# The second MLP product of a hybrid encoder block: four pairs of row blocks in one PSUM accumulation

## The chip, the cores and the metric

The kernel runs on one core of a Trainium2 chip. A core has a matrix engine (TensorE, PE in the rows), a vector engine (VectorE, DVE), a scalar engine (ScalarE, ACT), a general engine (GpSimd, POOL) and a queue that issues most transfers (SyncE, SP). Each executes its own instructions in order and waits for the others on semaphores. SBUF is the working memory of 128 partitions, PSUM the memory into which TensorE accumulates: eight banks, each of 512 float32 per partition. The metric is the device time of one execution in microseconds (us), lower is better; the time before is a median of three runs.

## What is computed

An encoder block over 1024 tokens of width 1024: two attention branches on a normed input, gated and merged, then an MLP with a squared ReLU and a final norm. The change touches the last part alone:

```
    merged = jax.nn.sigmoid(ga) * ya + jax.nn.sigmoid(gb) * yb
    x = x + merged @ w_out[l]

    h2 = rms_norm(x, norm_mlp_g[l], NORM_EPS)
    x = x + jnp.square(jax.nn.relu(h2 @ w_ff1[l])) @ w_ff2[l]
return rms_norm(x, norm_final_g, NORM_EPS)
```

`w_ff1` is 1024 x 4096 and `w_ff2` 4096 x 1024, all in float32.

## The kernel before

**The second product.** Call F the squared ReLU (1024 tokens x 4096). The first MLP product leaves F transposed in DRAM, `f_d[n][a]` being 128 rows of it by 1024 tokens; n counts 16 pairs of such row blocks, a = 0, 1 within a pair. One pair of F (split in token halves i and in a) and the matching 256 rows of `w_ff2` (split in a and in column halves) are two 2 x 2 block matrices, and the kernel multiplies them with seven block products instead of eight: products 1 to 7, of which 5, 6, 3 and 7 take a sum or difference of F blocks, and 5, 6, 4 and 7 a difference of weight blocks. The last two pairs (14, 15) are multiplied directly, in `last_product`.

**Operands.** Each float32 operand block is split into two parts, hi (a copy by ACT, rounded to the type float32r) and lo (the rest, a subtraction by DVE or POOL), in `operand` (L1245 to L1250). One block product is then three matmuls, hi x hi, hi x lo, lo x hi (L1291 to L1293), each with a 128 x 128 stationary block and 512 moving columns. `fa` are the operands from F, `wb` those from the weights, `fs` the combinations of F blocks (DVE, in `combine`, L1254) and `ws` those of weight blocks (POOL, the same line).

**Groups.** `ff2_group` (L1257) takes two pairs at a time, seven groups in all. For each of the seven products, in the order 1, 5, 6, 3, 4, 2, 7, it prepares the operands of both pairs and then runs four accumulations j (one for each block of 128 tokens of a half), each six matmuls into one PSUM bank. The four banks of a product alternate with the next product's: four banks as two tiles of two ("S"), and four as single tiles ("T", "T", "mm", "gm"). DVE then adds each bank into a running sum in SBUF (L1301); ACT copies instead in the first group's products 1, 5 and 6 (L1299). The running sums are the tiles `sum1`, `sum5`, `sum6` and, for the other products, quarters of the result: `xb` (first four token blocks, reloaded from DRAM by L1278) and `acc` (the other four). L1334 to L1342 put the sums together at the end, 28 instructions on DVE and POOL.

**Loads.** `pair_raws` (L1225) loads a pair of F as one tile of 128 x 2048 (`fr`, three buffers over two pools) and the weight rows as two tiles of 128 x 1024 (`w2r`, three buffers each).

**Order and memory.** The program is written in the order above, but a scheduler places each engine's instructions, and tiles come free when their last reader is done. Pools lie in SBUF as on two stacks. The pool `p52` (left) follows the operands of the first MLP product, the pools `p5` and `p5r` what lay on the right, among it the tiles `c` whose stores to `f_d` are the last step of the first MLP product (`squared`, L1141). Before the change the hi and lo operands lie in `p52`, and `fs` and `ws` in `p5r`.

Of the kernel before, what the change touches and what calls it, by code (L numbers as in the profile page):

```python
# [11 lines left out]
F32 = mybir.dt.float32  # L12
# [7 lines left out]
P = 128  # L20
# [63 lines left out]
def tile_hybrid_block(ctx: ExitStack, tc: tile.TileContext, t: dict, out: bass.AP):  # L84
# [1135 lines left out]

    s52a = tc.tile_pool(name="s52a", bufs=1)
    p52 = s52a.__enter__()
    sums = {1: [p52.tile([P, 512], F32, tag=f"sum1{j}", name=f"sum1{j}") for j in range(4)]}

    def pair_raws(pairs):  # L1225

        fr, wr = {}, {}
        for n in pairs:
            pool, bufs = (p5r, 1) if n % 3 == 2 else (p52, 2)
            fr[n] = pool.tile([P, 2, S], F32, tag="fr", name=f"fr{n}", bufs=bufs)  # L1230
            wr[n] = [wp.tile([P, D], F32, tag=("wh", "wl")[a], name=f"w2r{n}_{a}", bufs=3) for a in range(2)]
# [171 lines left out]
```

## Time and profile before

| | us |
|---|---|
| median of 3 runs | 1702.39 (1696.2 to 1707.07) |
| the profiled execution | 1701.56 |
| its span, first to last instruction | 1699.8 |
| busy in the span: PE, DVE, ACT, POOL | 1569.3, 1230.8, 709.4, 712.4 |
| matmuls of the seven groups, first and last start | 1335.5, 1640.6 |

Shares over the whole span mix stages with different limits, so the stage from 1335 to 1700 is read by itself: which engine is busy all the time there, and what TensorE waits for. Two durations are told apart: that of one instruction, and the pace, the time from one start to the next, which is shorter, since instructions of one engine overlap a little (a matmul's end is modelled and overlaps the next one by much).

### The profile page before, as it was taken

What the parts mean: (1) busy time and instruction counts of PE and PEld (TensorE: products, weight loads), DVE (VectorE), ACT (ScalarE), POOL (GpSimd) and SP (SyncE); (2) the same over time, 40 slices, a digit from 0 to 9 for tenths busy, and PEclk for the clock granted to TensorE, in tenths of its full rate; (3) what the DMA queues carried; (4) which work ended last, traced back from release to release, by engine and by line L of the source; (5) the groups of instructions that cost most, each with busy time, mean ns of one, the idle gap of its engine ahead of it and who ended that gap; (6) DMA issues with size and microseconds to landing.
All of it is one profiled execution on the core that took longest, in us unless ns stands there. A gap on an engine that the chain in (4) does not pass through costs nothing. (4 is left out here: it accounts for less than half of the span.)

```text
span 1699.8 us, 22314 instructions
## 1 busy us (share of the span) xinstructions
PE 1569.3 (92%) x8216; PEld 1324.2 (78%) x8216; DVE 1230.8 (72%) x1560; ACT 709.4 (42%) x1176; POOL 712.4 (42%) x412
## 2 busy tenths in 40 slices
PE   7899989998889998999999998999999888999997
PEld 6798767776677778899879996777888677777776
DVE  5876788689688996555546548544344899999995
ACT  4432222222567774445422336345444643333322
POOL 1634545455223241112120016333333498888771
PEclk8999999999899998999999999999999999999999
DMA  6366576555855658665475432433332632222212
GB/s 203 130 207 211 169 227 227 166 179 175 267 192 191 230 192 276 186 203 187 144 250 184 137 96 73 147 120 115 113 112 93 248 137 99 99 100 99 87 38 99
DMA packets 211869, 272.36 MB, mean 160 GB/s; under 512 B 12304, under 2 KB 146608, under 8 KB 211760
## 3 DMA queue, kind: packets, MB, share of 16 engines
q1 hardware_dynamic: 207152, 254.16, 46.0%
q10 hardware_dynamic: 4608, 16.78, 2.5%
q8 instruction: 65, 1.06, 0.3%
q14 instruction: 44, 0.36, 0.1%
HBM read 184.86 MB, written 80.27 MB: 156 GB/s over the span
## 5 line engine op out<-in xcount | busy, mean ns | idle before, releaser
L1291 PE MATMUL p<-wb_h,fa_h 128*128 128x512 f32 x392 | 157.1, 402 | 21.5 <-DVE xb L1301 8.1
L1292 PE MATMUL p<-wb_l,fa_h 128*128 128x512 f32 x392 | 155.8, 397 | 4.2 <-DVE wb_l L1249 4.2
L1293 PE MATMUL p<-wb_h,fa_l 128*128 128x512 f32 x392 | 155.3, 397 | 0.0
L1291 PEld LDWEIGHTS p<-wb_h,fa_h 128*128 128x128 f32 x392 | 74.9, 191 | 44.4 <-issue 14.5
L1249 POOL TENSOR_TENSOR wb_l<-ws,wb_h 128x512 fp32r<-128x512 f32 x54 | 86.0, 1603 | 17.3 <-ACT wb_h L1248 17.3
L1292 PEld LDWEIGHTS p<-wb_l,fa_h 128*128 128x128 f32 x392 | 75.5, 193 | 20.7 <-DVE wb_l L1249 5.2
L1293 PEld LDWEIGHTS p<-wb_h,fa_l 128*128 128x128 f32 x392 | 75.3, 192 | 16.5 <-DVE fa_l L1249 0.5
L702 ACT ACTIVATE p<-sb,mn 128x1024 f32<-128x1024 f32 x64 | 71.4, 1117 | 38.3 <-DVE mn L700 24.1
L697 PE MATMUL sb<-kb,qb 128*128 128x512 f32 x256 | 74.7, 416 | 13.1 <-ACT p L702 7.6
L700 DVE TENSOR_REDUCE mn<-sb 128x1 f32<-128x1024 f32 x64 | 76.7, 1216 | 11.0 <-PE sb L697 10.7
L1249 POOL TENSOR_TENSOR wb_l<-w2r,wb_h 128x512 fp32r<-128x512 f32 x48 | 78.7, 1660 | 13.7 <-ACT wb_h L1248 13.7
L164 POOL TENSOR_SCALAR n_y<-n_ss 128x1 f32<-128x1 f32 x23 | 6.0, 261 | 186.1 <-ACT n_xn L171 183.1
L273 DVE TENSOR_TENSOR s<-w 128x512 f32<-128x512 f32 x15 | 13.5, 901 | 97.2 <-DMA w<-in_w_ff 97.2
L254 POOL TENSOR_TENSOR wt_f_l<-w,wt_f_h 128x1024 fp32r<-128x1024 f32 x15 | 36.1, 2408 | 91.6 <-ACT wt_f_h L253 91.6
L1248 ACT ACTIVATE fa_h<-fs 128x512 fp32r<-128x512 f32 x56 | 35.1, 627 | 84.9 <-issue 40.9
L1249 DVE TENSOR_TENSOR fa_l<-fs,fa_h 128x512 fp32r<-128x512 f32 x56 | 70.4, 1264 | 0.0
L811 PE MATMUL sa<-kh_a,zq 128*128 128x256 f32 x256 | 69.2, 301 | 0.0
L1248 ACT ACTIVATE fa_h<-fr 128x512 fp32r<-128x512 f32 x50 | 31.2, 626 | 90.7 <-PE p L1292 52.2
L836 DVE TENSOR_TENSOR pta<-ta,pta 128x512 fp32r<-128x512 f32 x64 | 43.8, 688 | 33.7 <-ACT pta L835 33.4
L697 PEld LDWEIGHTS sb<-kb,qb 128*128 128x128 f32 x256 | 46.4, 194 | 25.4 <-ACT p L702 11.2
L811 PE MATMUL sa<-kl_a,zq 128*128 128x256 f32 x256 | 66.1, 289 | 0.0
L1142 ACT ACTIVATE c<-c 128x512 f32<-128x512 f32 x64 | 39.6, 623 | 56.2 <-DVE c L300 50.1
(500 smaller groups left out, 5272.1 us busy)
## 6 DMA issues: line engine op xcount, KB each, us to landing
w<-in_w_in SPq DMA_DIRECT2D x32, 512.0 KB, 4.2
qk<-r ACTq DMA_DIRECT2D x32, 512.0 KB, 4.5
f<-c SPq DMA_DIRECT2D x64, 256.0 KB, 4.6
w2r<-in_w_ff SPq DMA_DIRECT2D x32, 512.0 KB
fr<-f SPq DMA_DIRECT2D x32, 512.0 KB, 6.2
w<-in_w_ff SPq DMA_DIRECT2D x30, 512.0 KB
vb<-vb SPq DMA_DIRECT2D x16, 512.0 KB, 6.9
rot<-raw SPq DMA_DIRECT2D x64, 128.0 KB, 3.8
```

The source lines that it names most:

```text
L254: eng.tensor_tensor(lo[:, :n, :], x, f(hi[:, :n, :]), op=ALU.subtract)
L697: nc.tensor.matmul(sps[:, 512 * n:512 * n + 512], q[:, z, (qb % 4) * P:(qb % 4 + 1) * P], o.k[m][:, 512 * n:512 * n + 512], start=z == 0, ...
L700: nc.vector.tensor_reduce(mn, sps, axis=AX.X, op=ALU.min)
L702: nc.scalar.activation(p, sps, AF.Exp, scale=-1.0, bias=mn, accum_out=o.zz[qb][:, m:m + 1])
L811: nc.tensor.matmul(ps[:, 0:CM], zq[:, n % 4, c, :], kk[:, c * CM:(c + 1) * CM], start=c == 0 and kk is o.kh, stop=c == NCLS - 1 and kk is ...
L836: nc.vector.tensor_tensor(view[1], tv, f(view[0]), op=ALU.subtract)
L1142: nc.scalar.activation(c, c, AF.Relu)
L1248: nc.scalar.activation(hi, x, AF.Copy)
L1249: eng.tensor_tensor(lo, x, f(hi), op=ALU.subtract)
L1291: nc.tensor.matmul(acc, ah[:, c], bh, start=i == 0, stop=False)
L1292: nc.tensor.matmul(acc, ah[:, c], bl, start=False, stop=False)
L1293: nc.tensor.matmul(acc, al[:, c], bh, start=False, stop=i == len(ops) - 1)
```

## The change

Two pairs become one operand tile, "two pairs wide" (128 x 2 x 512): hi, lo, `fs` and `ws` are made for two pairs in one instruction. Pairs 0 and 1 are a group by themselves; after it three groups take four pairs each, so that an accumulation is twelve matmuls. The product order is 1, 5, 6, 3, 7, 2, 4. Products 6, 3 and 4 don't begin a new accumulation: they go on in the banks of products 1, 5 and 7, after DVE or ACT has read these. `sum1` falls away, and what is put together at the end is four instructions of 128 x 2048. Running sums are whole tiles, and where a bank tile is two banks wide, one instruction reads both.

All `ws` move from POOL to DVE, and so do the lo parts of the weights in product 1 (`nc.vector if which == 1 ...`). Operand tiles move from `p52` to `p5` on the right, four buffers of double width for eight; the F blocks and weight blocks are loaded by block (i, j) into single-buffered tiles `ra`, `rb` in `p52` (`rb00` in another pool), with rows of 512 elements.

```diff
-    def combine(eng, x, y, op, tag, name):
-        r = p5r.tile([P, 512], F32, tag=tag, name=name, bufs=6)
-        eng.tensor_tensor(r, x, y, op=op)
-        return r
...
+        def load_a(i, j):
+            r["a", i, j] = p52.tile([P, GROUP, 512], F32, tag=f"ra{i}{j}", name=f"ra{i}{j}_{pairs[0]}")
+            for g, n in enumerate(pairs):
+                nc.sync.dma_start(r["a", i, j][:, g, :], f_d[n][j][:, 512 * i:512 * i + 512])
...
+        for kind, i, j in (("b", 0, 0), ("a", 0, 0), ("b", 0, 1), ("a", 1, 0), ("a", 1, 1), ("b", 1, 1), ("a", 0, 1), ("b", 1, 0)):
+            (load_a if kind == "a" else load_b)(i, j)
...
     def operand(x, tag, name, eng):
-        hi = p52.tile([P, 512], F32R, tag=tag + "h", name=name + "_h", bufs=8)
-        lo = p52.tile([P, 512], F32R, tag=tag + "l", name=name + "_l", bufs=8)
+        hi = p5.tile([P, 2, 512], F32R, tag=tag + "h", name=name + "_h", bufs=4)
+        lo = p5.tile([P, 2, 512], F32R, tag=tag + "l", name=name + "_l", bufs=4)
         nc.scalar.activation(hi, x, AF.Copy)
         eng.tensor_tensor(lo, x, f(hi), op=ALU.subtract)
...
+    PRODUCTS = ((1, 0), (5, 0), (6, 1), (3, 1), (7, 0), (2, 0), (4, 1))
...
-                u = combine(nc.gpsimd, x, y, ALU.subtract, "t", f"ws{which}_{n}")
...
+                nc.vector.tensor_tensor(u, x, y, op=ALU.subtract)
+            return operand(s, "a", f"fa{name}", nc.vector), operand(
+                u, "b", f"wb{name}", nc.vector if which == 1 or begin and which == 5 else nc.gpsimd)
...
+                    nc.tensor.matmul(acc, ah[:, i % 2, c], bh[:, i % 2, :], start=i == 0 and not more, stop=False, skip_group_check=bool(more))
...
-                    for d, a in reads:
-                        if pairs[0] == 0 and which in (1, 5, 6):
-                            nc.scalar.activation(d, a, AF.Copy)
-                        else:
-                            nc.vector.tensor_tensor(d, a, d, op=ALU.add)
...
+                if begin and which in (5, 6):
+                    nc.scalar.activation(to, of, AF.Copy)
+                else:
+                    nc.vector.tensor_tensor(to, of, to, op=ALU.add)
...
+    s52 = tc.tile_pool(name="s52", bufs=1, side="right")
...
+    ff2_group((0, 1), raws, 0)
+    g_fin = load_gain(p5, t["norm_final_g"], "g_fin")
+    for count, n in enumerate(range(2, NP2 - 2, GROUP)):
+        pairs = tuple(range(n, n + GROUP))
+        ff2_group(pairs, pair_raws(pairs), count + 1)
...
+    for x in (res[0][:, :, 512:1024], res[1][:, :, 0:512], sums[5]):
+        nc.vector.tensor_tensor(x, x, sums[6], op=ALU.add)
+    nc.vector.tensor_tensor(res[1][:, :, 512:1024], res[1][:, :, 512:1024], sums[5], op=ALU.add)
```

**Where instructions stand: ScalarE, at the seam between the two MLP products.** Before, the hi parts of the first group (`fa_0_h`, `fa_1_h`, `wb_1_h`) stand among the last steps on the tiles `c` (relu L1142, square L1143):

```order
L266 ACTIVATE p_15_11835<-f0f_11837 128x512 [waits PE_49]
L1248 ACTIVATE fa_0_h<-fr_11868 128x512 [waits DMAHW2_49]
L1248 ACTIVATE fa_1_h<-fr_11871 128x512 [waits DMAHW3_49]
L1142 ACTIVATE c_15_11710<-c_15_11710 128x512 [waits DVE_49]
L1142 ACTIVATE c_15_11712<-c_15_11712 128x512 [waits DMAHW6_49,DVE_49]
L1143 ACTIVATE c_15_11710<-c_15_11710 128x512 [waits Activation_49]
L1143 ACTIVATE c_15_11712<-c_15_11712 128x512 [waits Activation_49]
L1142 ACTIVATE c_15_11711<-c_15_11711 128x512 [waits DMAHW5_49,DVE_49]
L1248 ACTIVATE wb_1_h<-w2r_0_11872 128x512 [waits DMAHW5_49]
L1143 ACTIVATE c_15_11711<-c_15_11711 128x512 [waits Activation_49]
```

In the changed program the same engine has them behind the last square, and the first one waits for seven transfer queues, PE and POOL at once:

```order
L1144 ACTIVATE c_15_11705<-c_15_11705 128x512 [waits Activation_49]
L1143 ACTIVATE c_15_11828<-c_15_11828 128x512 [waits DMAHW4_49,DVE_49]
L1144 ACTIVATE c_15_11828<-c_15_11828 128x512 [waits Activation_49]
L1261 ACTIVATE fa_0_h<-ra_0_11862 128x1024 [waits DMAHW2_49,DMAHW3_49,DMAHW1_49,DMAHW4_49,DMAHW0_49,DMAHW5_49,PE_49,DMAHW7_49,Activation_49,Pool_49]
L1261 ACTIVATE wb_0_h<-rb_0_11860 128x1024
```

In SP's order the seven queues are those of the seven last stores of `c` to `f_d`: the operand tiles now lie where `c` lay, and come free with these stores.

**VectorE in the middle of a group.** Before (group of pairs 2 and 3; `sum`, `xb` and `acc` rows are reads of banks, `fa_l` lo parts, `fs` combinations):

```order
L1254 TENSOR_TENSOR fs_4_12733<-fr_12673 128x512
L1301 TENSOR_TENSOR sum_11915<-p_2_0_12383,sum_11915 128x512
L1301 TENSOR_TENSOR sum_11916<-p_2_0_12383,sum_11916 128x512
L1249 TENSOR_TENSOR fa_2_l<-fr_12297,fa_2_h 128x512
L1301 TENSOR_TENSOR sum_11917<-p_2_1_12384,sum_11917 128x512
L1301 TENSOR_TENSOR sum_11918<-p_2_1_12384,sum_11918 128x512
L1301 TENSOR_TENSOR sum_11919<-p_2_0_12437,sum_11919 128x512
L1249 TENSOR_TENSOR fa_3_l<-fr_12300,fa_3_h 128x512
```

After (group of pairs 6 to 9, from the start of its product 5; the number in a name is the first pair of the two):

```order
L1290 TENSOR_TENSOR fs_6_12825<-fs_6_12825,ra_6_12728 128x1024
L1262 TENSOR_TENSOR fa_8_l<-fs_8_12837,fa_8_h 128x1024
L1297 TENSOR_TENSOR ws_6_12827<-rb_6_12746,ws_6_12827 128x1024
L1290 TENSOR_TENSOR fs_8_12837<-fs_8_12837,ra_6_12728 128x1024
L1329 TENSOR_TENSOR xb<-p_6_0_12773,xb 128x2x512
L1297 TENSOR_TENSOR ws_8_12839<-rb_6_12746,ws_8_12839 128x1024
L1262 TENSOR_TENSOR fa_6_l<-fs_6_12825,fa_6_h 128x1024
L1329 TENSOR_TENSOR xb<-p_6_1_12774,xb 128x2x512
L1262 TENSOR_TENSOR fa_8_l<-fs_8_12837,fa_8_h 128x1024
```

Reads of banks become fewer against operand work, `ws` rows stand between them, and every row is of double width.

**SyncE, the loads of the groups.** Before (pairs 6 and 7; `fr` are pairs of F, `w2r` rows of `w_ff2`, each tile with two or three buffers):

```order
L1238 DMA fr_13047<-f_9456 128x1024
L1240 DMA fr_13047<-f_9456 128x1024
L1234 DMA w2r_1_13049<-in_w_ff 128x1024
L1234 DMA w2r_0_13051<-in_w_ff 128x1024
L1234 DMA w2r_0_13424<-in_w_ff 128x1024
L1238 DMA fr_13050<-f_9457 128x1024
```

After (group of pairs 6 to 9; `ra_6_12741` is its block of F with i = 1, j = 1):

```order
L1236 DMA ra_6_12749<-f_9453 128x512
L1250 DMA rb_6_12754<-in_w_ff 128x2x512 x2
L1236 DMA ra_6_12741<-f_9450 128x512
L1236 DMA ra_6_12741<-f_9451 128x512
L1236 DMA ra_6_12741<-f_9452 128x512
L1236 DMA ra_6_12741<-f_9453 128x512
L1250 DMA rb_10_13261<-in_w_ff 128x2x512
```

Loads by pair have become loads by block; this one stands last in its group's loads and waits for the last reader of the same tile in the group ahead.

## Rows read from the trace of the kernel before

**Rows 1.** Busy time by stretch (start:end, length; PE, PEld, DVE, ACT, POOL; clock; DMA):

```profile
1250.00:1300.00 50.00, 50.00 (x220) 41.12 (x219) 25.03 (x37) 21.89 (x32) 16.85 (x7) 1.00 0.37 114
1335.40:1640.90 305.50, 279.77 (x1179) 223.83 (x1178) 304.76 (x352) 123.12 (x226) 256.02 (x160) 0.97 0.31 115
1640.90:1699.80 58.90, 45.69 (x193) 36.68 (x191) 37.31 (x38) 10.80 (x21) 17.75 (x24) 0.93 0.18 72
```

**Rows 2.** PE timeline, the first and the last of 130 matmuls without a stop:

```profile
1436.22 0.39 PE L1293 MATMUL p<-wb_h,fa_l 128*128 128x512 f32 x1
...
1465.50 0.39 PE L1293 MATMUL p<-wb_h,fa_l 128*128 128x512 f32 x1
```

**Rows 3.** Who waited for whom, TensorE, 1335.4 to 1640.9: total us, times, longest:

```profile
PE p L1291 <- DVE xb L1301: 8.1, 5, 2.9
PE p L1291 <- DVE acc L1301: 5.7, 5, 2.4
PE p L1291 <- ACT wb_h L1248: 5.3, 3, 3.8
PE p L1292 <- DVE wb_l L1249: 4.2, 2, 2.7
PE p L1291 <- DVE sum L1301: 2.4, 1, 2.4
```

**Rows 4.** Instructions by line and shape, 1200 to 1700: count, busy us, mean ns:

```profile
L1249 DVE TENSOR_TENSOR fa_l<-fs,fa_h 128x512 fp32r<-128x512 f32 x56 | 70.4, 1264 | 0.0
L1301 DVE TENSOR_TENSOR sum<-p,sum 128x512 f32<-128x512 f32 x72 | 46.2, 676 | 0.0
L1254 POOL TENSOR_TENSOR ws<-w2r,ws 128x512 f32<-128x512 f32 x28 | 46.8, 1692 | 14.3 <-DMA w2r<-in_w_ff 13.9
```

**Rows 5.** DVE and POOL timelines: start, length, instruction:

```profile
1461.31 1.78 DVE L1254 TENSOR_TENSOR fs<-fs,fr 128x512 f32<-128x512 f32 x1
1490.98 1.87 DVE L1301 TENSOR_TENSOR sum<-p,sum 128x512 f32<-128x512 f32 x3
...
1464.20 1.74 POOL L1249 TENSOR_TENSOR wb_l<-ws,wb_h 128x512 fp32r<-128x512 f32 x1
...
1483.91 1.28 POOL L1249 TENSOR_TENSOR wb_l<-ws,wb_h 128x512 fp32r<-128x512 f32 x1
```

**Rows 6.** Instructions of 1024 columns, timeline of DVE and ACT:

```profile
1317.25 1.22 DVE L254 TENSOR_TENSOR w1a_l<-w_last,w1a_h 128x1024 fp32r<-128x1024 f32 x1 [5.66 <-ACT w1a_h L253]
1318.39 0.68 DVE L297 TENSOR_TENSOR c<-yf,u 128x512 f32<-128x512 f32 x1
...
1682.64 1.22 DVE L1356 TENSOR_TENSOR acc<-ff_last,acc 128x1024 f32<-128x1024 f32 x1 [0.70 <-PE ff_last L1350]
...
1318.82 1.06 ACT L253 ACTIVATE w1a_h<-w_last 128x1024 fp32r<-128x1024 f32 x1 [1.12 <-PE zf L245]
```

**Rows 7.** Instructions by line and shape, POOL, 1000 to 1335, DVE idle much of the time:

```profile
L254 POOL TENSOR_TENSOR w1a_l<-w,w1a_h 128x1024 fp32r<-128x1024 f32 x7 | 16.8, 2396 | 17.7 <-ACT w1a_h L253 17.7
```

**Rows 8.** The seam: timelines of ACT, POOL and SP, and a transfer's time to landing:

```profile
1332.91 0.58 ACT L266 ACTIVATE p<-f0f 128x512 f32<-128x512 f32 x1
1335.47 1.14 ACT L1143 ACTIVATE c<-c 128x512 f32<-128x512 f32 x2
...
1335.74 3.13 POOL L1254 TENSOR_TENSOR ws<-w2r 128x512 f32<-128x512 f32 x2 [21.48 <-PE f1f L245]
...
f<-c SPq DMA_DIRECT2D x19, 256.0 KB, 2.8
```

**Rows 9.** Busy time by stretch: the loads ahead of the seam, the restart of TensorE, the next loads:

```profile
1325.00:1330.00 5.00, 5.00 (x23) 4.04 (x22) 2.26 (x5) 2.47 (x5) 0.00 (x0) 1.00 0.92 327
...
1340.00:1345.00 5.00, 3.86 (x9) 3.09 (x10) 5.00 (x6) 2.75 (x6) 4.17 (x4) 0.50 0.70 257
...
1350.00:1355.00 5.00, 4.67 (x21) 3.86 (x21) 5.00 (x5) 3.76 (x8) 4.64 (x3) 1.00 1.03 420
```

**Rows 10.** PE timeline: restarts after a wait, and the pace behind the first:

```profile
1341.14 0.80 PE L1292 MATMUL p<-wb_l,fa_h 128*128 128x512 f32 x1 [2.70 <-DVE wb_l L1249]
...
1342.16 0.63 PE L1291 MATMUL p<-wb_h,fa_h 128*128 128x512 f32 x1
1342.59 0.63 PE L1292 MATMUL p<-wb_l,fa_h 128*128 128x512 f32 x1
...
1646.95 0.80 PE L1349 MATMUL ff_last<-wb_l,fa_h 128*128 128x512 f32 x1 [3.71 <-POOL wb_l L1249]
...
1660.50 0.50 PE L1348 MATMUL ff_last<-wb_h,fa_h 128*128 128x512 f32 x1 [1.82 <-DVE xb L1356]
```

More of the change, by code (lines that the diff above doesn't have):

```diff
@@ L1304, in tile_hybrid_block, with ff2_group, block, fresh @@
-    side = [0]
+    PRODUCTS = ((1, 0), (5, 0), (6, 1), (3, 1), (7, 0), (2, 0), (4, 1))
+    def ff2_group(pairs, r, count):
+        begin = pairs[0] == 0
+        couples = range(len(pairs) // 2)
+        temp = {}
+        def block(kind, i, j, c):
+            return r[kind, i, j, c]
+        def fresh(side, name, c):
+            temp[side, c] = wp.tile([P, 2, 512], F32, tag="wh" if side == "a" else "wl", name=name, bufs=3)
+            return temp[side, c]
+        def prepare(which, c):
+            name = f"{which}_{pairs[2 * c]}"
+            a = {1: (0, 0), 2: (0, 1), 4: (1, 1)}.get(which)
+            b = {1: (0, 0), 2: (1, 0), 3: (1, 1)}.get(which)
+            if a:
+                s = block("a", *a, c)
+            else:
+                s = fresh("a", f"fs{name}", c) if which in (5, 7) else temp["a", c]
+                x, y, op = {5: (block("a", 1, 0, c), block("a", 1, 1, c), ALU.add), 6: (s, block("a", 0, 0, c), ALU.subtract),
+                            3: (block("a", 0, 1, c), s, ALU.subtract), 7: (block("a", 0, 0, c), block("a", 1, 0, c), ALU.subtract)}[which]
+                nc.vector.tensor_tensor(s, x, y, op=op)
+            if b:
+                u = block("b", *b, c)
+            else:
+                u = temp["b", c] if which in (6, 4) else fresh("b" if which == 5 else "b7", f"ws{name}", c)
+                x, y = {5: (block("b", 0, 1, c), block("b", 0, 0, c)), 6: (block("b", 1, 1, c), u),
+                        4: (block("b", 1, 0, c), u), 7: (block("b", 1, 1, c), block("b", 0, 1, c))}[which]
+                nc.vector.tensor_tensor(u, x, y, op=ALU.subtract)
+            return operand(s, "a", f"fa{name}", nc.vector), operand(
+                u, "b", f"wb{name}", nc.vector if which == 1 or begin and which == 5 else nc.gpsimd)
+        target = {1: res[0][:, :, 0:512], 2: res[0][:, :, 0:512], 3: res[0][:, :, 512:1024], 4: res[1][:, :, 0:512],
+                  7: res[1][:, :, 512:1024], 5: sums[5], 6: sums[6]}
+        banks = [None, None]
+        for k, (which, more) in enumerate(PRODUCTS):
+            ops = [prepare(which, c) for c in couples]
+            if not more:
+                if (k + count) % 2:
+                    banks[k % 2] = [bank([P, 512], tag, f"p{which}_{pairs[0]}_{j}") for j, tag in enumerate(("T", "T", "mm", "gm"))]
+                else:
+                    banks[k % 2] = [bank2(f"p{which}_{pairs[0]}_{j}") for j in range(2)]
+            here = banks[k % 2]
+            for j in range(4):
+                wide = len(here) == 2
+                acc = here[j // 2][:, 512 * (j % 2):512 * (j % 2) + 512] if wide else here[j]
+                c = slice(j * P, j * P + P)
+                for i in range(len(pairs)):
+                    (ah, al), (bh, bl) = ops[i // 2]
+                    last = i == len(pairs) - 1
+                    nc.tensor.matmul(acc, ah[:, i % 2, c], bh[:, i % 2, :], start=i == 0 and not more, stop=False, skip_group_check=bool(more))
+                    nc.tensor.matmul(acc, ah[:, i % 2, c], bl[:, i % 2, :], start=False, stop=False, skip_group_check=bool(more))
+                    nc.tensor.matmul(acc, al[:, i % 2, c], bh[:, i % 2, :], start=False, stop=last, skip_group_check=bool(more))
+                if wide and j % 2 == 0:
+                    continue
+                to = target[which][:, j - 1:j + 1, :] if wide else target[which][:, j, :]
+                of = here[j // 2].rearrange("p (j n) -> p j n", j=2) if wide else acc
+                if begin and which in (5, 6):
+                    nc.scalar.activation(to, of, AF.Copy)
+                else:
+                    nc.vector.tensor_tensor(to, of, to, op=ALU.add)
```

111 lines of the change are left out of this document (29 added, 82 removed).

## Prediction, made before the changed kernel was timed

> **What bounds the kernel now.** I read the time by stretch first, then TensorE's waits, then the instructions of the engine that it waits for. In a stretch of the first MLP product TensorE is busy throughout and DVE half the time [rows 1]. In the seven groups, 1335.4 to 1640.9 (the last matmul with its pace), this turns round: DVE is busy 304.76 of 305.50 us, TensorE 279.77 [rows 1]. The reader is to see that TensorE's busy time hides the loss, as its matmuls overlap. So I take its pace: 130 matmuls in an unbroken run start 1436.22 to 1465.50, 0.227 us each [rows 2]. The groups have 7 x 7 x 4 x 6 = 1176 matmuls, 266.9 us at that pace: 38.6 of the 305.5 us are lost. Of these, 25.7 are waits that the trace names, and 16.2 of them end with a DVE read of a bank (L1301) [rows 3]; the rest is restarts and low clock. The stage is bound by DVE, which gives the banks back too late.
>
> Why is DVE full? One add from a bank takes 0.68 us, and three in a row 1.87, a pace of 0.60 [rows 4, 5]. The subtractions with both inputs in SBUF take 1.26 on average, for the same 512 columns [rows 4]. Single ones take 1.78 while POOL's run 1.74, where POOL alone needs 1.28 [rows 5]: the two wait for each other. For a period of two pairs DVE has 28 reads and 22 SBUF instructions, 50 x 0.60 = 30.0 us; the period is 305.5/7 = 43.6. The other 13.6 are waits for POOL, whose 22 instructions take 28 us by themselves: DVE stood still for 0.49 of POOL's time.
>
> **The change part by part, for one group of four pairs.**
>
> TensorE: 336 matmuls x 0.227 = 76.3 us, 10.9 a product. Their number, 1176, stays.
>
> Bank reads: 28 of 512 columns instead of 56. In one half of the products (single banks) four take 2.4 us at the pace of 0.60; in the other half two of 1024 columns take 1.22 each from start to end [rows 6], some 2.3 together. Seven products: 16.5 us, before 33.6.
>
> DVE's SBUF work: 14 `fa_l`, 8 `fs`, and now 8 `ws` and 2 `wb_l` of product 1, 32 instructions of 1024 columns. One lasts 1.22 with the next 1.14 behind it [rows 6]: 36.5 us (before, 44 x 0.60 = 26.4). DVE together: 53.0 us.
>
> POOL: 12 `wb_l` of 1024 columns at 2.40 [rows 7], 28.8 us, before 44 instructions and 56 us. If DVE stands still for the same 0.49 of that, it needs 53.0 + 14.1 = 67.1 us, under TensorE's 76.3; before, the same sum was 87.2. So TensorE becomes the bound of the group. ACT has 28 hi copies of 1.06 [rows 6], 30 us: no bound.
>
> The Trainium skill, page "SBUF — State Buffer", section "Who interferes with whom", says that of a DVE instruction with two SBUF inputs and a GpSimd instruction that reads SBUF the later one waits until the other is through. The trace agrees as far as 1.78 against 0.68 goes [rows 4, 5]. By that rule no fixed share protects DVE, and waits get longer with wider instructions; the first rival is worked out on that.
>
> Deadlines inside a group: four buffers of double width let ACT begin the operands of a product when the product two ahead of it ends, so one product time, 10.9 us, is there to make them. I walked through the group of pairs 6 to 9 with these prices, each POOL instruction holding DVE's SBUF work off. Product 5's operands are ready 9.4 us after product 1 has started, product 6's at 21.0 (wanted at 21.8 and, for its second two pairs, 23.6), product 7's and 2's in time; product 3's second `fa_l` is 1.1 us late, behind four `fs` and `ws` and two POOL instructions. I allow 1 to 3 us a group, take 2, and 0 as the lower bound.
>
> Loads: tiles `ra`, `rb` have one buffer, so a block's load waits for its last reader. The tightest is F block (1, 1): its last reader, product 4's second `fa_l`, ends 61.3 us into the group. Four transfers of 256 KB need 5 us at 257 to 420 GB/s with 2.8 to land the first [rows 8, 9]: there at 66.5. DVE wants it at 66.6. It is hidden by product 2 and the reads of its banks; without that cover DVE would stand, with product 1's lo parts behind it, and 9.2 us more of DVE work would follow before the next group can start at 77.3, some 1.5 us of slack. SP has nothing behind these loads but later loads.
>
> The seam: operand tiles now wait for the last store of `c`. Before, TensorE goes from the last `f1f` matmul straight into product 1. Now: the last `p` is there at 1333.5 [rows 8]; three adds of 0.60 and an `fs` of 1.14 on DVE bring 1336.5, the last add from its bank 1337.2 (the `f1f` product is through by 1335.7 [rows 8]); relu and square, 1.14 for two [rows 8], 1338.3; four stores issued by 1339.9, the last landed 2.8 later [rows 8], 1342.7; two hi copies, 1344.8; `fa_l` and `wb_l`, 1346.0. TensorE stands 1335.4 to 1346.0: 10.6 us. Bounds: 8.6 if the stores issue as the tiles come, 14 if the loads ahead (full DMA rate [rows 9]) hold up `fs`. After its first wait of 2.7 us in the trace the granted clock was 0.50, that is 1.2 GHz, and matmuls came every 0.43 us, about twelve of them [rows 9, 10]; I count the same, 12 x 0.20 = 2.4. In the small group (pairs 0, 1) products last 5.4 us; DVE has 17 SBUF instructions (19.4), 5 products of reads (11.8) and 5 POOL instructions to wait for (6), 37 against 38.1 on TensorE: 1 us of loss.
>
> Sum of the groups' loss: 10.6 + 2.4 + 1 + 3 x 2 = 20.0, before 38.6: 18.6 us gained.
>
> The last part: before, TensorE waits there 3.7 us on POOL's `wb_l`, behind two POOL sums, and 1.8 on DVE, behind the 28 combining instructions [rows 10]. Now four instructions of 2048 columns on DVE, some 2.3 us each, three of them under the last products. The weights' lo parts of the second column half can begin only when product 4 ends: ready 5.4 and 9.0 us after it, wanted at 3.0 and 6.8, so 4.7 us of waits. Gain 1 (0 to 3).
>
> 1699.8 - 18.6 - 1 = 1680.2 of span. The profiled execution took 1.8 more than its span, and the median of the runs is 0.8 above it: **1683 us**.
>
> **Rivals.**
>
> *DVE stays the bound.* If every POOL instruction holds DVE for its whole length, a group needs 53.0 + 28.8 = 81.8 us, 5.5 more than TensorE instead of the 2 allowed, 3 x 3.5 = 10.5, and the widest waits shift product 3, 6 and 7 by about a microsecond each: 1693 to 1697. For it: the doubled length of POOL's instructions, and margins of about 1 us in the walk. Against: a third of DVE's work reads PSUM, and such reads keep 0.68 next to a busy POOL [rows 4].
>
> *Slower: the single buffers of the loads.* If block (1, 1) lands late, DVE stands in order and all operands behind it. From 68 us into the group each us late is one on TensorE, at four seams (three groups and the last part). To be 17 us slower than before it must cost 37 us, 9.3 a seam: landing 16 us after issue instead of 5. For it: one buffer in place of three. Against: 1 MB would have to move at 75 GB/s, where the trace has 420 in a stretch of such loads [rows 9]. Time: 1720.
>
> *Better.* No loss inside the groups, 8.6 at the seam, 3 gained at the end: 1671.
>
> **How the numbers follow.** About 1% (17 us) is what a measurement of this kernel can tell from no change. TensorE as the bound, 1676 to 1690: 0.62, of which 0.50 lies under 1685.4, that is over 1% faster. Better: 0.08. DVE as the bound: 0.24, all within 1%. Slower: 0.06. Faster 0.58, within 1% 0.36, slower 0.06. The range runs from the better case to the upper end of the first rival, 1670 to 1697; the likeliest case alone is 1676 to 1690.
>
> **What would show it.** Right: in the three groups TensorE's starts are 0.227 us apart over whole products, DVE is busy some 0.88 instead of 1.00, and waits on bank reads (16.2 us before) are nearly gone. The seam shows TensorE idle for about 10 us until an ACT copy that waited for a store, and a clock of 0.50 behind it. The rivals would show as DVE busy all through with TensorE waiting for `fa_l` or `wb_l`, or as DVE idle on `ra` at the end of each group. I am wrong if the share of POOL's time that DVE waits is far from 0.49, or if the first operands come much later than 1346.

## The result, and the profile after

The changed kernel takes 1675.28 us (median of four runs, 1673.88 to 1676.8) where the kernel before takes 1702.14: a ratio of 0.9844, 95% interval 0.9811 to 0.9877. That is 1.6% faster. The forecast was 1683, with a range of 1670 to 1697 and most of its chance on a gain of over 1%.

DVE is VectorE and POOL is GpSimd. The profiled execution took 1675.33 us, with a span of 1673.5. Busy time of the changed kernel by stretch (start:end, length; PE, PEld, DVE, ACT, POOL; clock; DMA), the first two to be laid beside [rows 1]:

```profile
1332.40:1619.40 287.00, 271.86 (x1178) 223.45 (x1178) 264.83 (x196) 110.24 (x118) 129.43 (x43) 0.97 0.35 119
1619.40:1673.50 54.10, 44.20 (x193) 35.62 (x191) 28.81 (x22) 11.95 (x21) 13.38 (x19) 0.97 0.19 78
...
1400.00:1600.00 200.00, 200.00 (x884) 165.62 (x883) 191.00 (x143) 74.89 (x76) 98.56 (x33) 1.00 0.29 98
...
1343.80:1349.00 5.20, 4.89 (x11) 3.40 (x12) 5.20 (x6) 2.21 (x4) 0.00 (x0) 0.50 0.98 371
...
1386.50:1396.50 10.00, 10.00 (x37) 8.09 (x38) 10.00 (x10) 2.01 (x2) 2.41 (x1) 0.83 0.17 54
```

And one stretch of the kernel before, for the third of them:

```profile
1400.00:1600.00 200.00, 185.09 (x794) 148.62 (x792) 200.00 (x240) 74.37 (x136) 170.69 (x107) 0.99 0.28 103
```

In the same 200 us in the middle of the groups TensorE now starts 884 matmuls instead of 794, 0.226 us each, and is never idle. DVE has turned from the engine that is always busy (200.00) into one with 9 us to spare. The groups went from 305.5 to 287.0 us and the last part from 58.9 to 54.1; the remaining 3 us lie ahead of the last `f1f` matmul (run 10 comes back to them). Of the runs of the kernel before that were taken beside the experiments, one took 3038.01 us and is left out.

All restarts of TensorE in the changed kernel from there to the middle of the last part (PE timeline, idle time in brackets):

```profile
1332.20 0.40 PE L245 MATMUL f1f<-hB,w1a_l 128*128 128x512 f32 x1
...
1343.88 1.22 PE L1319 MATMUL p<-wb_h,fa_h 128*128 128x512 f32 x2 [11.28 <-DMA rb<-in_w_ff]
1345.33 0.80 PE L1320 MATMUL p<-wb_l,fa_h 128*128 128x512 f32 x1 [0.23 <-DVE wb_l L1262]
...
1348.48 0.63 PE L1321 MATMUL p<-wb_h,fa_l 128*128 128x512 f32 x1
1348.91 0.63 PE L1319 MATMUL p<-wb_h,fa_h 128*128 128x512 f32 x1
...
1380.88 0.47 PE L1319 MATMUL p<-wb_h,fa_h 128*128 128x512 f32 x1 [1.08 <-DVE acc L1329]
1386.41 0.50 PE L1319 MATMUL p<-wb_h,fa_h 128*128 128x512 f32 x1 [2.55 <-DVE acc L1329]
...
1619.11 0.39 PE L1321 MATMUL p<-wb_h,fa_l 128*128 128x512 f32 x1
...
1626.93 0.50 PE L1364 MATMUL ff_last<-wb_last_l,fa_last_h 128*128 128x512 f32 x1 [2.69 <-POOL wb_last_l L1262]
```

From 1386.41 to the last product at 1619.11 there is not one restart: three groups at TensorE's own pace. The 16.2 us of waits on bank reads of [rows 3] are down to 3.6, all of them ahead of that stretch. Most of what is left of the loss stands at the seam, where the operands wait for the stores of `c`; the trace puts TensorE's wait down to a load that had long landed, and ACT's wait, in the second row, names the store (who waited for whom; total, times, longest):

```profile
PE p L1319 <- DMA rb<-in_w_ff: 11.3, 1, 11.3
ACT fa_h L1261 <- DMA f<-c: 5.4, 1, 5.4
PE p L1319 <- DVE acc L1329: 3.6, 2, 2.5
PE ff_last L1364 <- POOL wb_last_l L1262: 2.7, 1, 2.7
```

How DVE and POOL hold each other now, by line and shape, 1332.4 to 1673.5 (count, busy us, mean ns), beside [rows 4]:

```profile
L1262 POOL TENSOR_TENSOR wb_l<-ws,wb_h 128x1024 fp32r<-128x1024 f32 x27 | 79.3, 2952 | 151.9 <-ACT wb_h L1261 112.1 <-DMA g_fin<-in_norm_final_g 39.8
L1262 DVE TENSOR_TENSOR fa_l<-fs,fa_h 128x1024 fp32r<-128x1024 f32 x28 | 57.4, 2053 | 1.8 <-ACT fa_h L1261 1.8
L1329 DVE TENSOR_TENSOR xb<-p,xb 128x512 f32<-128x512 f32 x24 | 16.0, 678 | 0.0
L1329 DVE TENSOR_TENSOR xb<-p,xb 128x1024 f32<-128x1024 f32 x12 | 14.6, 1214 | 0.3 <-PE p L1321 0.3
```

The bank reads cost what they were priced at (0.68 and 1.21 us beside a busy POOL), while a subtraction out of SBUF that lasts 1.22 alone has a mean of 2.05.

### The profile page after: what moved, and what is told of

It reads as the page before. It is cut to its first block, busy times and chain, and to the rows that moved or that the text cites. A ratio compares the mean times of both kernels' runs of the same rounds, so it can differ in the third digit from the quotient of the medians.

```text
span 1673.5 us, 21830 instructions
## 1 busy us (share of the span) xinstructions
PE 1555.3 (93%) x8216; PEld 1318.4 (79%) x8216; DVE 1185.1 (71%) x1389; ACT 695.8 (42%) x1064; POOL 574.4 (34%) x287
## 5 line engine op out<-in xcount | busy, mean ns | idle before, releaser
L1319 PE MATMUL p<-wb_h,fa_h 128*128 128x512 f32 x392 | 154.6, 395 | 14.9 <-DMA rb<-in_w_ff 11.3
L1262 POOL TENSOR_TENSOR wb_l<-ws,wb_h 128x1024 fp32r<-128x1024 f32 x27 | 79.3, 2952 | 151.9 <-ACT wb_h L1261 112.1
L1261 ACT ACTIVATE fa_h<-fs 128x1024 fp32r<-128x1024 f32 x28 | 29.6, 1056 | 95.9 <-PE p L1320 63.2
L1143 ACT ACTIVATE c<-c 128x512 f32<-128x512 f32 x64 | 39.8, 624 | 55.7 <-DVE c L300 50.0
L824 ACT ACTIVATE sm<-sm,mna 128x512 f32<-128x512 f32 x64 | 46.1, 720 | 32.2 <-DVE mna L820 31.8
L1262 DVE TENSOR_TENSOR fa_l<-fs,fa_h 128x1024 fp32r<-128x1024 f32 x28 | 57.4, 2053 | 1.8 <-ACT fa_h L1261 1.8
L835 ACT ACTIVATE pta<-ta 128x512 fp32r<-128x512 f32 x64 | 37.7, 592 | 50.3 <-PE ta L831 42.7
```

The source lines that it names most:

```text
L824: nc.scalar.activation(sm, sm, AF.Exp, scale=-1.0, bias=mn, accum_out=stat[h % 2][:, n:n + 1])
L1143: nc.scalar.activation(c, c, AF.Relu)
L1319: nc.tensor.matmul(acc, ah[:, i % 2, c], bh[:, i % 2, :], start=i == 0 and not more, stop=False, skip_group_check=bool(more))
```

## The experiments

Nine kernels stand beside the two. Each ratio is to the runs of the kernel before that were taken beside that kernel, whose medians are 1700.93 to 1702.87 us. The count is that of matmuls started from 1400 to 1600 us, and the last column is DVE's busy time there. A profile is of one execution, whose time can lie some us off the median: 1713.05 in run 1, 1701.65 in run 2, 1723.40 in run 5, 1676.99 in run 8.

| kernel | us, median | ratio to before (95%) | matmuls | DVE busy |
|---|---|---|---|---|
| before | 1702.14 | 1 | 794 | 200.00 |
| changed | 1675.28 | 0.9844 (0.9811 to 0.9877) | 884 | 191.00 |
| 1: groups of two | 1723.2 | 1.013 (1.0105 to 1.0154) | 739 | 185.55 |
| 2: groups of two, two load buffers | 1707.05 | 1.0016 (1.0000 to 1.0032) | 772 | 196.50 |
| 3: groups of two, `ws` on POOL | 1707.84 | 1.0035 (1.0015 to 1.0056) | 810 | 185.56 |
| 4: `ws` on POOL | 1683.43 | 0.989 (0.9861 to 0.9919) | 872 | 183.89 |
| 5: before, `ws` on DVE | 1717.38 | 1.0073 (1.0040 to 1.0106) | 720 | 200.00 |
| 6: no operand work on POOL | 1665.74 | 0.9789 (0.9769 to 0.9809) | 884 | 179.62 |
| 7: the same, groups of two | 1692.45 | 0.9934 (0.9908 to 0.9959) | 811 | 196.11 |
| 8: early operands at the seam | 1669.79 | 0.9818 (0.9785 to 0.9851) | 873 | 191.66 |
| 9: 6 and 8 together | 1656.12 | 0.9728 (0.9700 to 0.9756) | 884 | 179.71 |

(In kernels 4 and 8 TensorE has a few waits in that stretch, 1.71 and 1.86 us of them named. With the slower starts around them the starts come 2.6 and 2.5 us late, 12 and 11 matmuls: what they lack against 884.)

**1. Groups of two row blocks' pairs**, the rest of the change as it is.

```diff
-    GROUP = 4
+    GROUP = 2
```

> The changed kernel with GROUP = 2: products of two row blocks' pairs share a bank again, and everything else of the change stays (operands two pairs wide, ws combinations on VectorE, products that go on in another's bank). **Theory (the halved bank reads made the gain):** a stretch of four pairs of the changed kernel has 16.5 us of bank reads and 36.5 us of SBUF work on VectorE, 53.0, and was seen 72.5 us busy with the lock; twice the bank reads make 72.5 + 16.5 = 89.0 us against 76.5 us of TensorE, so VectorE is the bound again and the three stretches give back 3 x 12.5 = 37 us: 1712 us (1703 to 1720), with VectorE busy over 0.97 of the stage and idle time of TensorE on bank reads. **Rival (the wide instructions, the moved combinations and the end of the part made it):** those are all still there, so the time stays within 10 us of 1675.

Measured: 1723.2 us, 48 above the changed kernel and over the expected 1703 to 1720. In the profiled execution (1713.05) the groups took 324.8 us, from 1326.6 to 1651.4, 37.8 more than in the changed kernel, against the 37 expected. The rival falls: with every other part of the change in place the gain is gone. But DVE was not the full 0.97 busy:

```profile
1400.00:1600.00 200.00, 178.25 (x739) 141.12 (x737) 185.55 (x162) 60.30 (x61) 75.91 (x26) 0.97 0.29 96
```

It stood idle 14.4 us there, and its waits from 1400 to 1600 say on what:

```profile
PE p L1319 <- DVE acc L1329: 11.1, 6, 3.7
...
DVE fs L1290 <- DMA ra<-f: 7.5, 5, 2.7
DVE ws L1297 <- POOL wb_l L1262: 6.9, 4, 2.3
```

So groups of two halve the time for the loads as well as doubling the reads, and the run mixes the two. That asked for the next one.

**2. Groups of two with two buffers for the loads** (the blocks are half as large there, so that they fit).

```diff
-            r["a", i, j] = p52.tile([P, GROUP, 512], ..., name=f"ra{i}{j}_{pairs[0]}")
+            r["a", i, j] = p52.tile([P, GROUP, 512], ..., name=f"ra{i}{j}_{pairs[0]}", bufs=2)
...
-                        whole = p52.tile([P, GROUP, 512], ..., name=f"rb{i}{j}_{pairs[0]}")
+                        whole = p52.tile([P, GROUP, 512], ..., name=f"rb{i}{j}_{pairs[0]}", bufs=2)
```

> Groups of two as in the first of these runs (ws on VectorE, low parts of the weights on GpSimd), and the raw blocks ra and rb, which are half as large there, with two buffers each, so that a block's load need not wait for its last reader. **Theory (the bank reads make nearly all of the loss of groups of two):** in the 200 us from 1400 that kernel started 739 matmuls where the changed one started 884, a loss of 32.8 us, and VectorE waited for loads 7.5 us of it; over the seven groups that is at most 10 us: 1713 us (1708 to 1719). **Rival (the loads, with one buffer and half the time, made the loss):** 1675 to 1690.

Measured: 1707.05 us. That is a little under the expected 1708 to 1719. The loads were worth 16 us of the 48 (19 by the two ratios), more than the 10 that the waits in the trace had shown; the other 32 stay with the doubled bank reads. DVE is nearly full again:

```profile
1400.00:1600.00 200.00, 184.59 (x772) 147.89 (x771) 196.50 (x173) 63.84 (x64) 76.17 (x27) 0.97 0.28 92
```

This kernel has the wide operands, the moved `ws` and the products that go on in another's bank, and is level with the kernel before (1.0016). Taken together, those parts gain nothing without the halved reads, which they make possible. What each is worth by itself this run doesn't say.

**3. Groups of two, and `ws` on POOL as before.**

```diff
-    GROUP = 4
+    GROUP = 2
...
-                nc.vector.tensor_tensor(u, x, y, op=ALU.subtract)
+                nc.gpsimd.tensor_tensor(u, x, y, op=ALU.subtract)
```

> The changed kernel with groups of two and ws on GpSimd: what is left of the change is the wide operands, the new loads, and products that go on in another's bank. **Theory (only the halved bank reads pay; the rest is even or costs a little):** not faster than the kernel before; with 0.49 to 0.69 of standing still for GpSimd's 48 us of four pairs, VectorE comes to 33 + 27.4 + 23.5 to 33 = 84 to 93 us against 87.2 of the kernel before, 1695 to 1725. **Rival (the wide operands make the gain and the move of ws hid it in the kernel with groups of two):** under 1690.

Measured: 1707.84 us, 0.35% slower than the kernel before and 15 us faster than run 1: the move of `ws` had cost those 15 us. The rival's time, under 1690, did not come, but this kernel has the single load buffers, and DVE waits 12.3 us for `ra` from 1400 to 1600. Groups of two with `ws` on POOL and two load buffers were not run, so that the wide operands by themselves are no gain is not shown.

**4. Groups of four, `ws` on POOL.**

```diff
-                nc.vector.tensor_tensor(u, x, y, op=ALU.subtract)
+                nc.gpsimd.tensor_tensor(u, x, y, op=ALU.subtract)
```

> The changed kernel with the eight ws combinations of four pairs back on GpSimd, where the kernel before had them. **Theory (bank reads; the move of ws is a trade that costs VectorE little either way):** VectorE loses 8 x 1.14 = 9.1 us of its own and GpSimd gains 8 x 2.40 = 19.2 us, 48 us in all; with 0.69 us of standing still for each us of GpSimd, as the changed kernel shows it, VectorE comes to 43.9 + 33 = 77 us against 76.5 of TensorE, a tie: 0 to 5 us per stretch of four pairs lost, 1675 to 1690. **Rival (the move of ws off GpSimd is what made the gain):** most of the 26 us goes back, 1693 to 1702.

Measured: 1683.43 us. 18.7 us of the gain remain, so the move of `ws` is not its cause. In the middle TensorE nearly keeps its pace, with two waits of 1.48 and 0.23 us. The profile shows where most of the loss within the groups is, at the start of the first product:

```profile
1347.99 1.22 PE L1319 MATMUL p<-wb_h,fa_h 128*128 128x512 f32 x2 [13.18 <-DMA rb<-in_w_ff]
1351.61 0.79 PE L1320 MATMUL p<-wb_l,fa_h 128*128 128x512 f32 x1 [2.40 <-DVE wb_l L1262]
```

These two waits are 4.1 us longer than in the changed kernel, and the groups, 291.0 us, are 4.0 longer. Of the other 4 us of the profile, 2.2 lie ahead of the seam, where the edit changes nothing.

**5. The kernel before with `ws` on DVE**, one part of the change alone.

```diff
-                u = combine(nc.gpsimd, x, y, ALU.subtract, "t", f"ws{which}_{n}")
+                u = combine(nc.vector, x, y, ALU.subtract, "t", f"ws{which}_{n}")
```

> The kernel before with one part of the change alone: its ws combinations (512 columns wide) on VectorE in place of GpSimd. **Theory (with VectorE as the bound this is a trade):** for two row blocks' pairs VectorE takes over 8 x 0.60 = 4.8 us and GpSimd gives up 8 x 1.28 = 10.2 us, for which VectorE stood still 0.49 to 0.69 of the time, 5.0 to 7.1 us: from 0.2 us slower to 2.3 us faster per two pairs, 1686 to 1706 in all. **Rival A (the move makes the gain of the change):** 1675 to 1685. **Rival B (VectorE does not win back the lock, the added work is paid in full):** 7 x 4.8 = 34 us slower, 1730 to 1740.

Measured: 1717.38 us, 0.73% slower, which fits none of the three. Its groups took 321.8 us in the profile, 16.3 more than before, 2.3 for each two pairs. Of the 4.8 us that DVE takes over, it won back about half, where I had expected all of it. So the price of the lock is not a fixed share of POOL's time: the 10.2 us of POOL work that went gave back some 2.5 us, 0.24 of it, not 0.49. (The profiled execution is 6 us above the median, so 2.5 is rather too little.) The move costs where DVE is full or nearly so (this run, 200.00 of 200 us busy; run 1 against run 3, 185.55 and idle only on loads and POOL) and pays where DVE has time to spare (the changed kernel against run 4). That this is the reason is inferred from these pairs.

**6. No operand work on POOL.**

```diff
-                u, "b", f"wb{name}", nc.vector if which == 1 or begin and which == 5 else nc.gpsimd)
+                u, "b", f"wb{name}", nc.vector)
...
-    blocks_b = {(i, j): operand(r["b", i, j, 0], "b", f"wb_last{i}{j}", nc.gpsimd) ...
+    blocks_b = {(i, j): operand(r["b", i, j, 0], "b", f"wb_last{i}{j}", nc.vector) ...
```

> The changed kernel with the low parts of the weight operands (wb_l, wb_last_l) on VectorE in place of GpSimd, which then has no operand work in the stage. **Theory (VectorE's busy time of 72.5 us is 53.0 of work and 19.5 of standing still behind GpSimd):** VectorE takes over 12 x 1.14 = 13.7 us and loses the 19.5, so 66.7 us of four pairs, 0.87 of TensorE's 76.5; the steady stretches stay at TensorE's pace and give nothing, but the stalls that a held VectorE makes (1.08 and 2.55 us ahead of the first stretch of four pairs with about 2 us of low clock behind, 2.69 us on wb_last_l in the last part) go or shrink: 3 to 8 us faster than the changed kernel, 1667 to 1672. **Rival (the seconds on VectorE are real work and GpSimd's help is worth it):** VectorE comes to 72.5 + 13.7 = 86 us and the stage gets 28 us longer, about 1704.

Measured: 1665.74 us, 9.5 below the changed kernel, a little more than forecast. DVE does 12 instructions more in a group and is less busy:

```profile
1400.00:1600.00 200.00, 200.00 (x884) 165.62 (x883) 179.62 (x172) 70.98 (x73) 0.00 (x0) 1.00 0.30 100
```

179.62 of 200 us are 68.5 of a group's 76.3, against the 66.7 that the prices gave. This run has the lock out of the way and confirms the prices of DVE's own work within 3%. After the first product's two waits (11.51 and 0.23 us) the trace names no wait of TensorE up to the end of the last part's products. In the last part, DVE's big sums take their own time again (DVE timeline of this kernel, then of the changed one):

```profile
1616.03 1.22 DVE L1262 TENSOR_TENSOR wb_last_l<-rb,wb_last_h 128x1024 fp32r<-128x1024 f32 x1
1617.16 2.29 DVE L1356 TENSOR_TENSOR acc<-acc,sum 128x2048 f32<-128x2048 f32 x1
```

```profile
1620.90 3.78 DVE L1356 TENSOR_TENSOR acc<-acc,sum 128x2048 f32<-128x2048 f32 x1
1624.60 3.36 DVE L1262 TENSOR_TENSOR fa_last_l<-ra,fa_last_h 128x1024 fp32r<-128x1024 f32 x1
```

**7. The same in groups of two**, with two buffers for the loads: the bank reads with no lock in play.

```diff
-    GROUP = 4
+    GROUP = 2
```

> Groups of two with two buffers for the raw blocks, and the low parts of the weight operands on VectorE, so that GpSimd has no operand work and nothing holds VectorE; to be compared with the same kernel in groups of four (1665.7). **Theory (VectorE's own work, bank reads among it, against TensorE's):** four pairs cost VectorE 33 + 36.5 + 13.7 = 83.2 us against 76.3 of TensorE, 3 x 6.9 = 21 us, and a backlog of up to 7 us goes into the last part: 1686 to 1694, VectorE busy over 0.97 in the stretch from 1400 to 1600. **Rival (the lock with GpSimd, not the bank reads, made VectorE the bound):** without it groups of two cost no more than groups of four, 1664 to 1670.

Measured: 1692.45 us, inside the theory's 1686 to 1694, 26.7 us above run 6.

```profile
1400.00:1600.00 200.00, 187.04 (x811) 151.07 (x809) 196.11 (x204) 66.09 (x65) 0.00 (x0) 1.00 0.31 103
```

DVE is busy 0.98 with GpSimd's part of the row at zero. So in this form of the kernel, with POOL's work on DVE, twice the reads are enough to make DVE the bound without any lock. It was otherwise in the kernel before: by the prediction's prices DVE's own work was 30.0 us for two pairs, against 168 x 0.227 = 38.1 of TensorE, and only with the 13.6 us of waiting for POOL did it become the bound. There it was the reads and the lock together; the kernel before without POOL's operand work was not run (estimate: 22 instructions x 0.60 more on DVE, 43.2 us, no gain). TensorE's named wait in that stretch is 12.3 us on `wb_l` of DVE, not on a bank: a full DVE is late wherever its order puts the lateness.

**8. The first two products' operands in space that is free at once** (the sum buffers, and the halves of `ra` that the small group leaves empty), so that they need not wait for the last store of `c`.

```diff
-    def operand(x, tag, name, eng):
+    def operand(x, tag, name, eng, into=None):
...
+            if begin and which == 1:
+                ia, ib = [[early[w][:, h:h + 2, :] for h in (0, 2)] for w in (5, 6)]
+            elif begin and which == 5:
+                ia, ib = [[p52.tile([P, 2, 512], F32R, tag=f"ra{i}{j}1", ...) for j in range(2)] for i in range(2)]
```

> The changed kernel with the operands of the first two products of the first, small group in space that is free before the last store of c (the two sum buffers and the unused halves of the ra buffers), so that they do not wait for that store. **Theory (TensorE's 11.3 us at the seam are the wait for the store of c, through the space that the operands take):** product 1 starts within 3 us of the last f1f product, it and product 5 take 2 x 24 x 0.227 = 10.9 us in which the store lands, and a rest of 1 to 3 us stays ahead of product 6; the clock does not fall, which saves another 2 us: 7 to 11 us faster, 1664 to 1668. **Rival (the store itself comes later, since four ACT copies of 1.06 us and four VectorE subtractions of 1.14 us now run ahead of the squares that it waits for):** the idle time moves from product 1 to product 6 and 0 to 4 us are gained, 1671 to 1675.

Measured: 1669.79 us, 5.5 below the changed kernel, under the 7 to 11 expected and over the rival's 4. TensorE goes straight on from the last `f1f` product at 1337.35 to product 1 at 1337.58, which shows the cause of the 11.3 us. But three waits come behind, and their sum is 7.6 us:

```profile
1351.92 0.79 PE L1329 MATMUL p<-wb_h,fa_h 128*128 128x512 f32 x1 [3.27 <-ACT fa_h L1264]
1355.16 0.80 PE L1330 MATMUL p<-wb_l,fa_h 128*128 128x512 f32 x1 [2.45 <-POOL wb_l L1265]
1359.55 0.80 PE L1331 MATMUL p<-wb_h,fa_l 128*128 128x512 f32 x1 [1.89 <-DVE fa_l L1265]
```

Of them only the first goes back to the store (in ACT's order, where the copy at 1347.00 waits 0.44 us for it). The store itself comes later, as the rival had it: the last square on `c` ends 7.0 us after the last `f1f` product (1337.58), against 4.0 in the changed kernel (ACT timeline):

```profile
1343.95 0.63 ACT L1144 ACTIVATE c<-c 128x512 f32<-128x512 f32 x1
```

The other two are POOL and DVE, which hold each other there, and a fourth of the kind, 1.86 us, comes at 1425; I had counted the first alone. The clock fell all the same, a mean of 0.66 over 1348 to 1360. With it, TensorE's starts come 12.7 us late by 1368, where in the changed kernel they are 14.6 late by 1353 (both against 0.2265 us a start): at the seam itself the edit won 2 us. The groups took 281.8 us in the profile, 5.2 less than in the changed kernel, because the changed kernel's two waits at the end of the small group (5.8 us with the low clock behind) are gone as well, less 2.6 at 1425.

**9. Both edits together.** The edit is that of runs 6 and 8.

> The changed kernel with both of the last two edits: the first two products' operands in space that is free at once, and the low parts of the weight operands on VectorE. **Theory (the seam and the lock are two costs, and the second is also what kept the first edit below its forecast: of the 11.3 us at the seam 7.6 came back as waits of 3.27 on the store, 2.45 on GpSimd and 1.89 us on a held VectorE):** the last two of these go with GpSimd out of the stage, some 3 us of waiting on the store stays, and the clock does not fall: 5 to 9 us below the 1665.7 of the kernel without GpSimd, 1657 to 1661. **Rival (both edits remove the same stalls):** the gains do not add, 1663 to 1667.

Measured: 1656.12 us, 9.6 below run 6, a little beyond the 5 to 9. The clock fell here too (0.76 over 1345 to 1352), which I had not expected. One wait is left of the four:

```profile
1345.28 1.20 PE L1329 MATMUL p<-wb_h,fa_h 128*128 128x512 f32 x4 [2.93 <-ACT fa_h L1264]
```

At the seam TensorE's starts are 5.0 us late, against 12.7 in run 8. So the lock did eat most of run 8's gain there. This kernel beats both: 2.7% under the kernel before and 1.2% under the changed one.

**10. The kernel before once more.** No edit.

> The kernel before once more, for a second profile. **Theory (the 3 us by which the last f1f product ends earlier in the changed kernel, 1332.4 against 1335.3, are not of the change, since the code ahead of it is the same but for four GpSimd additions; the six profiles so far have the last f1f product anywhere from 1326.3 to 1337.4):** it starts somewhere else than at 1335.3 by 1 us or more, and the stretch from there to the last p product is 305 us again, within 2. **Rival (the change makes the part ahead of the seam shorter):** it starts at 1335 within 1 us.

Measured: one run of 1702.15 us, and the last `f1f` matmul stands where it stood:

```profile
1335.24 0.40 PE L245 MATMUL f1f<-hB,w1a_l 128*128 128x512 f32 x1
```

The expectation of another place missed; the stretch to the last product, 306 us, came as expected. The rival is right in part. The `f1f` matmuls with hi weights, first and last start, in the kernel before and in the changed one:

```profile
L245 PE MATMUL f1f<-hB,w1a_h x128: 392/396/397, 1007.8 to 1335.0; 128*128 128x512 f32 x128
L245 PE MATMUL f1f<-hB,w1a_h x128: 392/396/400, 1006.9 to 1332.0; 128*128 128x512 f32 x128
```

From the first to the last it is 327.2 us before, 327.7 in this run and 327.3 in run 5, but 324.3 to 326.3 in the changed kernel and the eight made from it. So about 2 of the 3 us go with the change. They are there within 43 us of the first start, where the kernel before has four POOL subtractions of blocks of the result (L1279, in `ff2_group`, placed that early) that the change drops, and that hold DVE (POOL and DVE, before; DVE, changed kernel):

```profile
1007.29 1.30 POOL L1279 TENSOR_TENSOR acc<-acc 128x512 f32<-128x512 f32 x1 [1.40 <-DVE n_xn L173]
...
1007.62 2.05 DVE L254 TENSOR_TENSOR w1a_l<-w1r,w1a_h 128x1024 fp32r<-128x1024 f32 x1
```

```profile
1006.73 1.23 DVE L254 TENSOR_TENSOR w1a_l<-w1r,w1a_h 128x1024 fp32r<-128x1024 f32 x1
```

That they are the whole of the 2 us was not tried by itself. The rest of the spread is not of the change: over all kernels here the last start lies at 1326.1 to 1337.1, and the first one already at 1001.0 to 1012.8.

## Why the prediction was right, point by point

**The bound.** Right. The groups were bound by DVE, through the reads of the banks on top of the waits for POOL, and halving the reads made TensorE the bound. Runs 1, 2 and 7 show it from the other side, with and without the lock: 32 us between run 2 and the changed kernel, 26.7 between runs 7 and 6.

**The sum of the groups' loss** was 20.0 us. It came out at 287.0 - 266.9 = 20.1, and the 18.6 us of gain at 18.5. That is closer than its terms deserve:

| term | predicted | measured |
|---|---|---|
| seam, TensorE idle | 10.6 | 11.28 + 0.23 |
| low clock behind it | 2.4 | 2.5 |
| first small group, up to 1386.41 | 1 | 1.08 + 2.55, and 1.7 of low clock |
| three groups of four pairs | 6 | 0 |

(The low clock: ten matmuls from 1343.88 to 1348.91 in 5.03 us, less 2.27 at the full pace and the 0.23; a clock of 0.83 over 10 us. The granted clock was 0.50, 1.2 GHz, from 1343.8 to 1349.0. The terms sum to 19.3; 0.8 are spread.)

The seam was right in its sum (first matmul forecast 10.6 us after the end of the `f1f` product, measured 11.45) and in its cause, but two of its steps were off, and they cancel by luck. The walk had the first hi copy 7.3 us after the `f1f` product; it came 9.4 after it (1332.43 to 1341.83). The squares ended 4.0 after it instead of 2.9, and the last store, issued at 1337.3, took about 4.5 us to the copy that waited for it, where 2.8 was forecast (ACT timeline, the last square and the first hi copy):

```profile
1335.83 0.63 ACT L1144 ACTIVATE c<-c 128x512 f32<-128x512 f32 x1
1341.83 1.06 ACT L1261 ACTIVATE fa_h<-ra 128x1024 fp32r<-128x1024 f32 x1 [5.37 <-DMA f<-c]
```

Against these 2.1 us, TensorE began right behind the two hi copies (1343.83) with hi x hi, where the walk had it wait 1.2 us more for the lo parts. The term for the groups was mis-sized by all of its 6 us. The walk let every POOL instruction hold all of DVE's SBUF work, and found product 3's second `fa_l` 1.1 us late; in the trace nothing of that arrived at TensorE. The small group's term was too small by 4. Ahead of its first wait (1.08) DVE stood 1.23 us for a load of `ra` into its single buffer, the first row of DVE below; ahead of the second (2.55) it lost its place through the lock (timelines of POOL and of DVE, changed kernel):

```profile
1381.74 2.40 POOL L1262 TENSOR_TENSOR wb_l<-ws,wb_h 128x1024 fp32r<-128x1024 f32 x1 [12.62 <-ACT wb_h L1261]
...
1437.48 3.41 POOL L1262 TENSOR_TENSOR wb_l<-rb,wb_h 128x1024 fp32r<-128x1024 f32 x1
```

```profile
1377.24 1.22 DVE L1290 TENSOR_TENSOR fs<-ra,ra 128x1024 f32<-128x1024 f32 x1 [1.23 <-DMA ra<-f]
...
1381.78 3.44 DVE L1290 TENSOR_TENSOR fs<-ra,ra 128x1024 f32<-128x1024 f32 x1
1385.14 1.21 DVE L1329 TENSOR_TENSOR acc<-p,acc 128x1024 f32<-128x1024 f32 x1
...
1438.54 3.43 DVE L1262 TENSOR_TENSOR fa_l<-ra,fa_h 128x1024 fp32r<-128x1024 f32 x1
```

POOL started 0.04 us earlier, DVE stood still until its 2.40 were over, and the read behind gave the bank back at 1386.35: TensorE restarts at 1386.41. In run 6, without POOL's work, the loads ahead are issued 9 us earlier (1360.99 instead of 1370.23) and neither wait is there.

**DVE's standing still.** The share of 0.49 was too low, which the prediction had named as a sign of being wrong; the bound held because a margin was left. DVE is busy 191.00 of 200 us, 72.9 of a group's 76.3 us or 0.95, where 67.1 or 0.88 was forecast. With run 6 for its own work (68.5 less the 12 x 1.14 that it took over, 54.8) it stood still 18.1 us of POOL's 28.8, 0.63. Had it been 0.75 the group would have turned to DVE's side (54.8 + 0.75 x 28.8 = 76.4). The first rival, that every POOL instruction holds DVE for its whole length, was right on the single instruction: the `fa_l` at 1438.54 ends 1.08 us after the `wb_l` that was there first. It was wrong on the sum, since part of POOL's time falls on reads of banks and on gaps. The Trainium skill, page "SBUF — State Buffer", section "Who interferes with whom", has the second of the two wait for the whole instruction of the first; these rows agree, 3.43 and 3.44 us against 1.22 alone.

**The last part.** Gain 4.8, forecast 1 (0 to 3): the term was mis-sized. TensorE waits 2.69 us for `wb_last_l` instead of the 4.7 forecast, though two of the sums of 2048 columns take 3.8 and 3.9 us instead of 2.3; and the clock in the part is 0.97 instead of 0.93. Run 1 has the same code there and needs 59.9 us, as long as before, with 7.30 us of wait on DVE's last bank read. So the fewer sums alone did not shorten the part; DVE also has to come into it without a backlog, which the sum for the groups had not carried over. Before, DVE's last bank read (the second of the first row) starts 4.5 us after the last product's last matmul (1640.59), in the changed kernel 1.1 us after it (1619.11):

```profile
1644.48 1.27 DVE L1301 TENSOR_TENSOR acc<-p,acc 128x512 f32<-128x512 f32 x2
```

```profile
1620.18 0.68 DVE L1329 TENSOR_TENSOR acc<-p,acc 128x512 f32<-128x512 f32 x1
```

How the 4.8 us divide between the two is not shown.

**The slower rival, loads in single buffers.** It did not happen, but for the 1.08 us at the end of the small group: in the middle stretch DVE waits 5.8 us on `rb` and none on `ra`, and TensorE does not feel it. Runs 1 and 2 show that it was a real danger, since in groups of two, with half the time for each load, one buffer instead of two cost 16 us.

**From span to median.** Forecast 1680.2 of span, measured 1673.5. Of these 6.7 us, 3.8 are the last part and 3 lie ahead of the seam, where the prediction had put the change at nothing; about 2 of them go with the POOL subtractions that it drops (run 10).

## What to carry to other kernels

Where an engine that empties the accumulators is the one that is always busy, price its work per matmul and ask first what makes it read less often: letting four blocks accumulate where two did was worth 27 to 32 us here, and everything else in the change, taken together, about nothing. Moving work between two engines that hold each other has to be judged anew in each form of a kernel, by which engine has time to spare: the same eight combinations cost 15 us in one grouping and gave 8 in the other, 2 of these ahead of the stage. And look at what a change drops, too: four small subtractions, placed by the scheduler 300 us ahead of the stage, seem to have cost 2 us there. When a stage is cured, add up what it used to hand on to the next one: backlog and low clock are where the forecast of the last part was off.

## What the runs showed of the hardware that I had not expected

- An engine can have less to do without its helper: DVE with 12 instructions more in a group was busy 179.62 of 200 us, and 191.00 with POOL's help.
- The loss to the lock is not proportional to the other engine's work. It was 0.49 of POOL's time in the kernel before and 0.63 after, and taking 10.2 us of POOL's work away (run 5) gave back only about 2.5.
- Kernels that differ only behind a point reach that point at different times: the nine that share the code up to the seam start their first `f1f` matmul at 1001.0 to 1012.8 us, over 300 us ahead of what differs, while two profiles of the kernel before agreed to 0.5 us there and to 0.02 us at the last. What moves it was not tried. From the first `f1f` matmul to the last, the same nine agree within 2 us.
